# A two-layer hybrid decoder on one core: parameter columns laid out by the host, loads and lower parts in order of use, one softplus chain in layer 0

## The chip, the cores and the metric

The kernel runs on one core of a Trainium2 chip. The metric is device microseconds for one launch; the program builds in one piece and is executed several times. A core has five engines with an instruction queue each, worked off in order: TensorE (PE, matmuls and transposes, with its weight loads PEld), VectorE (DVE), ScalarE (ACT), GpSimd (POOL) and SyncE (SP, which here only issues loads and stores). The engines wait for one another on semaphores.

## The reference

Two layers, each of three sub-layers between a norm in front and a norm behind, over 256 tokens of width 1024 in f32:

```
h = rms_norm(x, pre_mix_g);   x += rms_norm(mixer(h) , post_mix_g)
h = rms_norm(x, pre_cross_g); x += rms_norm(cross(h, rms_norm(mem)), post_cross_g)
h = rms_norm(x, pre_ffn_g);   x += rms_norm((silu(h@w_gate) * (h@w_up)) @ w_down, post_ffn_g)
```

The mixer projects h with one matrix `w_in` (1024 x 3080) whose columns belong to three head groups. The RG-LRU group runs a short convolution, two gates and a linear recurrence whose decay is `exp(-8 * r * softplus(-lambda))`. The forgetting attention adds to its logits the differences of `c = cumsum(log_sigmoid(f + b_f))`, one f per token and head (8 heads). The retention group rotates q and k by position and weights the scores by a fixed decay. The three outputs are concatenated and multiplied by `w_out`. `log_sigmoid(z)` is `-softplus(-z)`, so the f of both token tiles and lambda all pass through a softplus.

## The kernel before, in words

The 256 tokens are two tiles of 128 (t = 0 and 1). All large products are made in three passes of a rounded format: an f32 operand is split into an upper part (`hi`, a cast on ACT) and a lower part (`lo = raw - hi`, a subtraction on DVE, or on POOL for two pieces of the beginning), and `mm3` (L355) issues hi·hi, hi·lo and lo·hi. The normed activations are split likewise: `flip_half` (L601) transposes four 128-column blocks of x on PE, multiplies them by a gain column on DVE (`xg`), casts on ACT (`xth`), and `rest` (L611) subtracts on DVE (`xtl`). The factor of the norm per token (`rs`) is applied after the product, so the products need only the gains.

Weights stream through five raw buffers (`RAW_BUFS`, 1056 columns each) and eight pairs of split buffers. `load` (L423) issues the next load on SP as soon as the raw buffer's lower part has been taken, and `pump` (L433) issues the next split. The plan of pieces begins, in layer 0, with `fv_hi` (264 columns, four pieces of two k-blocks), `fk` (512 columns, four pieces), `lru` (four), `fv_lo` (two), `fq`, `rqk` and `rvg` (four each).

Everything is emitted by one Python program that carries a clock per engine, `Flow` (L117): each instruction is charged a duration (`Engine.cost`, L238, and `matmul`, L308), and side tasks (generators that were spawned) are resumed between two `mm3` as soon as the model says that what they wait for is ready. So the duration table sets where transposes, softmax pieces and small products stand in the queues of all engines, for the whole program.

The beginning before the change: SP loads a first part of a packed constant array (`cst`: identity, 16 rows of pre_mix gains, the forget bias and the inverse frequencies, 304 columns), x of tile 0 in two halves, two weight pieces, x of tile 1 in one load, and the other pieces. PE warms up on zeros (`busy`, L1163), transposes the 16 gain rows into columns (`cols`), then the blocks of x. In `project` (L481) each k-block's three passes follow one another. `second_tile` (L1186) flips tile 1 and then issues on POOL five loads: a second part of `cst` (triangle, ones and 72 more parameter rows), the mask, the third part of `cst` (1024 KB) and the two memory tiles (512 KB each). `setup_rest` (L1129) transposes the 72 rows and runs the softplus of lambda, four columns wide. `use_fv_hi` (L700) runs a softplus, eight columns wide, for the f of each tile, and multiplies its result with triangle and ones on PE (`cum`), on which the keys and queries of the attention wait (`augmented`, L719). A softplus is 15 dependent instructions on DVE, fourteen of them behind one Exp on ACT.

At a layer's end `post` normalises the last product of a tile, adds it to x, and flips x for the next sub-layer; PE meanwhile works on what it has.

Of the kernel before, what the change touches and what calls it, by code (L numbers as in the profile page):

```python
# [15 lines left out]
ALU = mybir.AluOpType  # L16
# [28 lines left out]

C_ID, C_R1, C_BF, C_INV, C_FIRST = 0, 128, 256, 272, 304
C_TRI, C_ONE, C_R2, C_SOON = 304, 432, 560, 688
C_DEC, C_BD, C_END = 688, 1712, 2736


G_MIX = 0
N_FIRST = 16
G_MEM, G_CROSS, G_FFN = 16, 24, 40
L_CW, L_CB, L_BR, L_BI, L_LAM = 56, 72, 76, 80, 84
N_ROWS = 88

# [15 lines left out]
def _pack(inp):  # L72

    (eye, tri, ones, dec, inv), mask = _constants()
    pack = np.zeros((P, C_END), np.float32)
    pack[:, C_ID:C_ID + P] = eye
    pack[:, C_TRI:C_TRI + P] = tri
    pack[:, C_ONE:C_ONE + P] = ones
    pack[:, C_DEC:C_BD] = dec
    pack[:, C_INV:C_FIRST] = inv  # L80
    pack[0:N_FIRST, C_R1:C_R1 + P] = inp["pre_mix_g"].reshape(-1, P)
    for r0, name in ((G_MEM, "mem_norm_g"), (G_CROSS, "pre_cross_g"), (G_FFN, "pre_ffn_g"), (L_CW, "conv_w"),
                     (L_CB, "conv_b"), (L_BR, "b_rg"), (L_BI, "b_ig"), (L_LAM, "lru_lambda")):
        v = inp[name].reshape(-1, P)
        pack[r0 - N_FIRST:r0 - N_FIRST + v.shape[0], C_R2:C_R2 + P] = v
# [31 lines left out]
class Flow:  # L117
# [6 lines left out]
    def __init__(self):  # L124
        self.clock = {"PE": 0.0, "ACT": 0.0, "DVE": 0.0, "POOL": 0.0, "DMA": 0.0}
        self.seq, self.tasks, self.pumps, self.written, self.hold = 0, [], [], {}, 0
        self.free, self.reads, self.late = {}, {}, []
# [29 lines left out]
    def load(self, queue, out):  # L157

        if queue == "POOL":
            self.issue("POOL", 1.05, [], [])  # L160
        t = max(self.now, self.clock.get(queue, 0.0), self.free.get(out.tensor.name, 0.0)) + 1.1
        cost = out.nbytes() / 370e3
# [50 lines left out]
class Engine:  # L213
# [24 lines left out]
    def cost(self, op, outs, ins, kw):  # L238
        n = max(_size(x) for x in outs + ins[:1])
        psum = any(x.space == bass.MemoryType.PSUM for x in outs + ins)  # L240
        if self.name == "ACT":
            f = ([x for x in kw["funcs"] if x in TABLES] or [self.table])[0]
            load, self.table = 1.3 * (TABLES.get(f) != TABLES.get(self.table)), f
            return load + (0.165 if psum else 0.2) + n * 0.82e-3 + 0.19 * ("accum_out" in kw) + 0.09 * (len(ins) - 1)
        if self.name == "POOL":
# [31 lines left out]
def decoder(ctx: ExitStack, tc: tile.TileContext, a, out):  # L277
# [21 lines left out]
    def small(shape, dt=F32, n="s"):  # L299
        return sp.tile(shape, dt, tag="s", name=nm(n), bufs=64)  # L300

# [26 lines left out]
    def softplus(out_ap, x, n):  # L328

        ab, e, d, w, w2, q = (small([P, n], n=k) for k in ("ab", "e", "d", "aw", "aw2", "aq"))  # L330
        V.scalar_tensor_tensor(ab, x, -1.0, x, op0=ALU.mult, op1=ALU.max)
# [148 lines left out]

    def project(x, b):  # L481

        q = bank("acc")
        for k in range(KC):
            wh, wl = weights(b, k, NT)
# [17 lines left out]
    ident, tri, ones = (cst[:, c:c + P] for c in (C_ID, C_TRI, C_ONE))  # L503
    rows1, rows2 = cst[0:N_FIRST, C_R1:C_R1 + P], cst[0:N_ROWS - N_FIRST, C_R2:C_R2 + P]
    bf = cst[:, C_BF:C_INV].rearrange("p (l h) -> p l h", l=DEPTH)
# [4 lines left out]
    minus_half = const([P, 4], n="mh")  # L510
    cols = const([P, N_ROWS], n="cols")
    posi = const([P, NT], I32, n="posi")
    cosb, sinb = const([P, NT, 32], n="cos"), const([P, NT, 32], n="sin")
    spl, hb = const([P, 8], n="spl"), const([P, 8], n="hb")
    sp2, sp4 = spl[:, 0:4], spl[:, 4:8]

    SY.dma_start(out=cst[:, 0:C_FIRST], in_=a["pack"][:, 0:C_FIRST])
    for c in range(2):
        SY.dma_start(out=X[0][:, 512 * c:512 * c + 512], in_=a["x"][0, 0:P, 512 * c:512 * c + 512])
    load(2)  # L520
    SY.dma_start(out=X[1], in_=a["x"][0, P:2 * P, :])
    load(RAW_BUFS)
# [170 lines left out]
    def mixer(l, xt, blk, skew):  # L693
# [6 lines left out]
        def use_fv_hi(t, q):  # L700
            S.activation(v[t][:, 256:512], q[:, 0:256], AF.Copy, bias=0.0, scale=rs[t])
            z, lf[t], cum[t] = small([P, 8], n="z"), small([P, 8], n="lf"), small([P, 8], n="cum")
# [5 lines left out]
            for s in range(t + 1):  # L708
                matmul(b[:, 0:8], tri if s == t else ones, lf[s], s == 0, s == t)
            V.tensor_copy(cum[t], b[:, 0:8])  # L710
            got["cum", t] = 1

# [415 lines left out]

    def setup_rest():  # L1129
        tb = bank("tr")  # L1130
        transpose(tb[:, 0:N_ROWS - N_FIRST], rows2)
        V.tensor_copy(cols[:, N_FIRST:N_ROWS], tb[:, 0:N_ROWS - N_FIRST])
        neg = small([P, 4])
        V.tensor_scalar(neg, cols[:, L_LAM:L_LAM + 4], -1.0, None, op0=ALU.mult)
        yield from softplus(sp2, neg, 4)
        PO.tensor_scalar(sp4, sp2, -4.0, None, op0=ALU.mult)
        PO.tensor_scalar(sp2, sp2, -2.0, None, op0=ALU.mult)
        V.tensor_scalar(hb, cols[:, L_BR:L_BR + 8], 0.5, None, op0=ALU.mult)

    def memory_norm(m):  # L1140
# [113 lines left out]
```

## Time and profile before

| | |
|---|---|
| median of 3 runs | 852.02 us (851.98 to 853.30) |
| the profiled execution: its own time | 851.84 us |
| its span, from first to last instruction | 850.1 us |
| PE busy | 838.3 us, 99% of the span |
| DVE, ACT, POOL busy | 556.5, 436.4, 77.0 us |
| mean granted PE clock | 0.997 |

Rows of a timeline give start, duration, engine, line, operation, output<-inputs, and in brackets how long the engine stood idle before it and what released it. A row with xN merges N instructions of the same kind. Matmuls are pipelined: a row's duration holds its latency too, so the distance between the starts of two rows is what PE takes for one.

### The profile page before, as it was taken

The numbers are of one execution on the slowest core, as the hardware profiler recorded it, in microseconds if no ns is written. First come the engines' busy times: TensorE is split into PE (matmuls) and PEld (weight loads), VectorE is DVE, ScalarE is ACT, GpSimd is POOL, SyncE is SP. The second block draws the span as 40 slices with busy tenths as digits, with TensorE's granted clock in tenths as the row PEclk, the third lists the DMA queues.
The fourth block names the chain that finished last, engine by engine and source line by source line (L and its number), as shares of the span: only waits on it lengthen the run. The fifth ranks groups of instructions, "written<-read, shape, count | busy, mean of one in ns | idle before, by whom it ended". The sixth has DMA issues, their size and how long they took to land.

```text
span 850.1 us, 13415 instructions
## 1 busy us (share of the span) xinstructions
PE 838.3 (99%) x5328; PEld 751.0 (88%) x5329; DVE 556.5 (65%) x812; ACT 436.4 (51%) x666; POOL 77.0 (9%) x121
## 2 busy tenths in 40 slices
PE   7999999999999999999999999999999999999997
PEld 5888998999889999999888889889988899999995
DVE  5877886865577655557585775687566874656552
ACT  5479565645456434435355764465455653534431
POOL 2831211100020000000010201010001100000000
PEclk9999999999999999999999999999999999999999
DMA  8863525763457747546435523646443676657411
GB/s 270 302 221 106 174 76 174 216 205 100 149 155 258 234 140 229 188 137 227 145 99 173 173 81 119 223 148 227 146 151 101 221 243 202 198 143 232 146 51 50
DMA packets 92623, 145.25 MB, mean 171 GB/s; under 512 B 4768, under 2 KB 62240, under 8 KB 92432
## 3 DMA queue, kind: packets, MB, share of 16 engines
q1 hardware_dynamic: 91120, 138.65, 51.2%
q0 software_dynamic: 1440, 5.74, 1.9%
q8 instruction: 42, 0.69, 0.3%
q14 instruction: 21, 0.17, 0.1%
HBM read 143.32 MB, written 1.05 MB: 170 GB/s over the span
## 4 chain that ended last, share of the span: by engine, by line
PE 96%; issue 1%; DMA 1%; DVE 0%; SPq 0%; ACT 0%; DVEq 0%; POOLq 0%; POOL 0%; ACTq 0%
PE acc L309 61%; PE dn L309 24%; PE tr L321 4%; PE lg L309 2%; PE clg L309 1%; PE co L309 1%; PE fo L309 1%; DMA raw<-in_w_in 1%; PE ry L309 1%; PE rsc L309 1%; SPq L229 0%; PE gate L309 0%; DVE xg L234 0%; ACT xth L234 0%; DVE lo L234 0%
## 5 line engine op out<-in xcount | busy, mean ns | idle before, releaser
L234 DVE TENSOR_TENSOR lo<-raw,hi 128x1024 fp32r<-128x1024 f32 (+1 forms) x244 | 292.0, 1219 | 151.1 <-ACT hi L234 150.3
L234 ACT CAST hi<-raw 128x1024 fp32r<-128x1024 f32 (+2 forms) x246 | 251.5, 1043 | 137.4 <-PE acc L309 93.7
L309 PE MATMUL acc<-xth,hi 128*128 128x256 f32 x704 | 198.9, 282 | 0.0
L309 PE MATMUL acc<-xth,lo 128*128 128x256 f32 x704 | 198.6, 282 | 0.0
L309 PE MATMUL acc<-xtl,hi 128*128 128x256 f32 x704 | 197.7, 281 | 0.0
L309 PEld LDWEIGHTS acc<-xth,hi 128*128 128x128 f32 x704 | 133.1, 189 | 0.8
L309 PEld LDWEIGHTS acc<-xtl,hi 128*128 128x128 f32 x704 | 133.0, 189 | 0.8
L309 PEld LDWEIGHTS acc<-xth,lo 128*128 128x128 f32 x704 | 133.1, 189 | 0.0
L309 PE MATMUL acc<-hi,xth 128*128 128x512 f32 (+2 forms) x288 | 111.5, 387 | 2.4 <-ACT xth L234 2.3
L309 PE MATMUL acc<-lo,xth 128*128 128x512 f32 (+2 forms) x288 | 106.9, 371 | 1.2 <-DVE lo L234 0.8
L309 PE MATMUL acc<-hi,xtl 128*128 128x512 f32 (+2 forms) x288 | 107.1, 372 | 0.2 <-DVE xtl L234 0.2
L309 PEld LDWEIGHTS acc<-hi,xth 128*128 128x128 f32 x288 | 54.9, 191 | 11.6 <-ACT xth L234 3.0
L309 PEld LDWEIGHTS acc<-hi,xtl 128*128 128x128 f32 x288 | 54.6, 190 | 10.3 <-DVE xtl L234 0.7
L309 PEld LDWEIGHTS acc<-lo,xth 128*128 128x128 f32 x288 | 55.0, 191 | 9.6 <-DVE lo L234 1.0
L234 POOL TENSOR_TENSOR rp<-ssp,mh 128x1 f32<-128x1 f32 x12 | 6.7, 560 | 545.2 <-DVE ssp L234 545.2
L309 PE MATMUL dn<-hi,mth 128*128 128x512 f32 x128 | 51.1, 399 | 0.0
L309 PE MATMUL dn<-hi,mtl 128*128 128x512 f32 x128 | 50.5, 394 | 0.0
L309 PE MATMUL dn<-lo,mth 128*128 128x512 f32 x128 | 50.4, 393 | 0.0
L309 PE MATMUL dn<-hi,gh 128*128 128x512 f32 x112 | 44.2, 395 | 0.0
L309 PE MATMUL dn<-hi,gl 128*128 128x512 f32 x112 | 44.1, 394 | 0.0
L309 PE MATMUL dn<-lo,gh 128*128 128x512 f32 x112 | 44.1, 393 | 0.0
L234 DVE TENSOR_TENSOR y<-dn,gpost 128x512 f32<-128x512 f32 x24 | 16.4, 686 | 34.1 <-ACT junk L234 34.1
(228 smaller groups left out, 1369.9 us busy)
## 6 DMA issues: line engine op xcount, KB each, us to landing
raw<-in_w_in SPq DMA_DIRECT2D x44, 512.0 KB, 4.5
raw<-in_w_gate SPq DMA_DIRECT2D x44, 512.0 KB, 4.5
raw<-in_w_up SPq DMA_DIRECT2D x44, 512.0 KB, 4.7
raw<-in_w_down SPq DMA_DIRECT2D x44, 512.0 KB, 4.5
raw<-in_w_ck SPq DMA_DIRECT2D x16, 512.0 KB, 4.4
raw<-in_w_out SPq DMA_DIRECT2D x16, 512.0 KB, 4.2
raw<-in_w_cv SPq DMA_DIRECT2D x16, 512.0 KB, 5.2
raw<-in_w_cq SPq DMA_DIRECT2D x16, 512.0 KB, 5.0
```

Source lines behind the costliest of these rows:

```text
L234: fn(*args, **kw)
L309: nc.tensor.matmul(out_ap, lhsT, rhs, start=start, stop=stop)
L321: nc.tensor.transpose(out_ap, src, ident[0:k, 0:k])
```

## The change

The host now lays all 88 parameter columns into `cst` as columns (C_COLS), so both transposes of parameter rows and the copies behind them go. The first load of `cst` has 136 columns (identity and pre_mix gains); the 384 columns of the second part (the other parameters, forget bias, frequencies, triangle, ones) are loaded on SP behind the fourth weight piece, not on POOL. x of tile 1 comes in two halves. In the beginning the lower parts are all made on DVE, two of them ahead of or between the lower parts of x, and the two uppers come first on ACT. `project` for the first product works piece by piece: both k-blocks hi·hi, then hi·lo, then lo·hi. In layer 0 the softplus of lambda and of both tiles' f is one chain on 20 columns, spawned with tile 1, and the three `cum` products follow it together; layer 1 keeps a chain for each tile. The duration table of `Flow` is lowered: DVE by 0.075 us for most instructions, ACT by 0.065 us, the hand-over between engines from 0.15 to 0.12 us, and the first loads are charged 270 instead of 370 KB per us.

```
-    def issue(self, engine, cost, outs, ins, latency=0.15):
+    def issue(self, engine, cost, outs, ins, latency=0.12):
...
-            return load + (0.165 if psum else 0.2) + n * 0.82e-3 + 0.19 * ("accum_out" in kw) + 0.09 * (len(ins) - 1)
+            return load + (0.1 if psum else 0.135) + n * 0.82e-3 + 0.19 * ("accum_out" in kw) + 0.09 * (len(ins) - 1)
...
-        return 0.155 + n * (0.6e-3 if one else 1.06e-3) + 0.06 * (op == "scalar_tensor_tensor" and not psum)
+        return 0.08 + n * (0.6e-3 if one else 1.06e-3) + 0.06 * (op == "scalar_tensor_tensor" and not psum)
...
+        for k0 in range(0, KC if staged else 0, b.per):
+            ks = range(k0, k0 + b.per)
+            w = {k: weights(b, k, NT) for k in ks}
+            for i, j in ((0, 0), (0, 1), (1, 0)):
+                for k in ks:
+                    matmul(q[:, 0:b.n], x[i][:, k, :], w[k][j], k + i + j == 0, k == KC - 1 and i == 1)
+                flow.tick()
...
-    load(2)
-    SY.dma_start(out=X[1], in_=a["x"][0, P:2 * P, :])
+    for t in range(NT):
+        for c in range(2):
+            cut = slice(512 * c, 512 * c + 512)
+            SY.dma_start(out=X[t][:, cut], in_=a["x"][0, t * P:t * P + P, cut])
+        load(2 + 2 * t)
+    SY.dma_start(out=cst[:, C_FIRST:C_SOON], in_=a["pack"][:, C_FIRST:C_SOON])
...
-            yield from softplus(lf[t], z, 8)
+            if skew:
+                yield from softplus(lf[t], z, 8)
+            elif t == 0:
+                return
+            else:
+                yield [cst[:, C_FIRST:C_SOON], z]
+                V.tensor_scalar(zs[:, 0:4], cols[:, L_LAM:L_LAM + 4], -1.0, None, op0=ALU.mult)
+                yield from softplus(lfs, zs, 20)
+                PO.tensor_scalar(sp4, lfs[:, 0:4], -4.0, None, op0=ALU.mult)
...
-    def setup_rest():
...
-    pump(True, lows)
+    for _ in range(2):
+        pump(True, lows)
     second = flip_half(nrm[0], X[0], G_MIX, 1)
     busy(WARM2)
+    lows[0](V)
     rest(*first)
-    lows[0](V)
+    lows[1](V)
     rest(*second)
-    for eng in (PO, V, PO):
-        pump(True, lows)
-        lows[-1](eng)
...
-        PO.dma_start(out=cst[:, C_FIRST:C_SOON], in_=a["pack"][:, C_FIRST:C_SOON])
...
-    flow.spawn(setup_rest(), rows2)
```

Place 1 is the beginning. On ACT, before: the four uppers of `fv_hi` (raw_86 to raw_93) and the first of `fk` (raw_95) all stand ahead of the two casts of tile 1 (xg_187, xg_200).

```order
L234 CAST hi_129<-raw_86 128x528
L234 CAST xth_99<-xg_137 128x512
L234 CAST hi_149<-raw_88 128x528
L234 CAST hi_155<-raw_91 128x528
L234 CAST hi_161<-raw_93 128x528
L234 CAST hi_177<-raw_95 128x1024
L234 CAST xth_99<-xg_187 128x512
L234 CAST xth_99<-xg_200 128x512
```

On ACT now: the third piece of `fv_hi` is raw_92, the fourth raw_94; tile 1's products are xg_177 and xg_189.

```order
L230 CAST hi_128<-raw_86 128x528
L230 CAST hi_133<-raw_88 128x528
L230 CAST xth_101<-xg_141 128x512
L230 CAST hi_167<-raw_92 128x528
L230 CAST xth_101<-xg_177 128x512
L230 CAST xth_101<-xg_189 128x512
L230 CAST hi_194<-raw_94 128x528
```

The casts of tile 1 moved ahead of the fourth upper and of the first `fk` piece. On DVE at the same place, before:

```order
L234 TENSOR_TENSOR lo_156<-raw_91,hi_155 128x528
L234 TENSOR_TENSOR lo_178<-raw_95,hi_177 128x1024
L234 TENSOR_TENSOR xg_187<-tr_182,cols_77 128x512
L234 TENSOR_TENSOR xg_200<-tr_195,cols_77 128x512
L234 TENSOR_TENSOR xtl_100<-xg_187,xth_99 128x512
L234 TENSOR_TENSOR xtl_100<-xg_200,xth_99 128x512
```

On DVE now, from the third lower part on:

```order
L230 TENSOR_TENSOR lo_168<-raw_92,hi_167 128x528
L230 TENSOR_TENSOR xg_177<-tr_172,cst_74 128x512
L230 TENSOR_TENSOR xg_189<-tr_184,cst_74 128x512
L230 TENSOR_TENSOR xtl_102<-xg_177,xth_101 128x512
L230 TENSOR_TENSOR xtl_102<-xg_189,xth_101 128x512
L230 TENSOR_TENSOR lo_195<-raw_94,hi_194 128x528
L230 TENSOR_TENSOR lo_208<-raw_97,hi_207 128x1024
```

Tile 1 now stands between the third and the fourth lower part, where before it stood behind the first lower part of `fk`; the second and fourth lower parts, which POOL made before, are on DVE.

Place 2 is the softplus of layer 0 on DVE. Before, the chain of tile 0 (e_281 to lf_276) follows the last lower part of `lru` (lo_368), and the chain of tile 1 follows it:

```order
L234 TENSOR_TENSOR lo_368<-raw_225,hi_367 128x1024
L234 TENSOR_SCALAR d_282<-e_281 128x8
L234 RECIPROCAL d_282<-d_282 128x8
L234 TENSOR_TENSOR aw_283<-e_281,d_282 128x8
L234 TENSOR_TENSOR aw_284<-aw_283 128x8
L234 TENSOR_SCALAR aq_285<-aw_284 128x8
L234 SCALAR_TENSOR_TENSOR aq_285<-aq_285,aw_284 128x8 x7
L234 SCALAR_TENSOR_TENSOR aq_285<-aq_285,aw_283 128x8
L234 SCALAR_TENSOR_TENSOR lf_276<-z_275,aq_285 128x8
```

Now the one chain (all its tiles are called soft_82) begins with lambda behind the last lower part of `lru` (lo_346), and its main part stands behind the first lower part of `fv_lo` (lo_377, of raw_281, the thirteenth piece):

```order
L230 TENSOR_TENSOR lo_346<-raw_262,hi_345 128x1024
L230 TENSOR_SCALAR soft_82<-cst_74 128x4
L230 SCALAR_TENSOR_TENSOR soft_82<-soft_82 128x20
L230 TENSOR_SCALAR aug_357<-acc_305,rstd_119 128x8x64
L230 MEMSET aug_357 128x8
L230 TENSOR_TENSOR lo_377<-raw_281,hi_376 128x1024
L230 TENSOR_SCALAR soft_82<-soft_82 128x20
L230 RECIPROCAL soft_82<-soft_82 128x20
```

One wide chain moved behind one more weight piece than the narrow ones had in front of them. On PE the three `cum` products stand together behind 75 matmuls of 512 columns (`fk` and `lru`); before, the first stood behind 72 and the other two behind 90.

Place 3 is PE at the change of layers, where tile 1's x is transposed (tr) for layer 1 while PE works on tile 0's `fk`, before tile 1's first product (acc_4642 before and acc_4573 now, 264 columns). Before:

```order
L321 MATMUL tr_4597<-cst_74,x_73 128x128 x4
L321 MATMUL tr_4605<-cst_74,x_73 128x128 x4
L309 MATMUL acc_4575<-hi_4487,xth_99 128x512
L309 MATMUL acc_4575<-lo_4488,xth_99 128x512
L309 MATMUL acc_4575<-hi_4487,xtl_100 128x512
L309 MATMUL acc_4642<-hi_4282,xth_99 128x264
```

And now:

```order
L317 MATMUL tr_4522<-cst_74,x_73 128x128 x4
L317 MATMUL tr_4530<-cst_74,x_73 128x128 x4
L305 MATMUL acc_4506<-hi_4414,xth_101 128x512
L305 MATMUL acc_4506<-lo_4415,xth_101 128x512
L305 MATMUL acc_4506<-hi_4414,xtl_102 128x512
L305 MATMUL acc_4506<-hi_4423,xth_101 128x512
L305 MATMUL acc_4506<-lo_4424,xth_101 128x512
L305 MATMUL acc_4506<-hi_4423,xtl_102 128x512
```

Three more matmuls like the last three follow before tile 1's first product, so nine matmuls, not three, stand between the transposes and it: the transposes moved up by six matmuls.

More of the change, by code (lines that the diff above doesn't have):

```diff
@@ L43 @@
 HOLD_LEAD = 1
[L46 to L53, printed above, removed]
+C_ID, C_COLS, C_FIRST = 0, 128, 136
+C_BF, C_INV, C_TRI, C_ONE, C_SOON = 216, 232, 264, 392, 520
+C_DEC, C_BD, C_END = 520, 1544, 2568
+G_MIX, G_MEM, G_CROSS, G_FFN = 0, 16, 24, 40
 L_CW, L_CB, L_BR, L_BI, L_LAM = 56, 72, 76, 80, 84
-N_ROWS = 88
 def _constants():
@@ L124, in __init__ @@
     def __init__(self):
-        self.clock = {"PE": 0.0, "ACT": 0.0, "DVE": 0.0, "POOL": 0.0, "DMA": 0.0}
+        self.clock = {"PE": 0.0, "ACT": 0.0, "DVE": 0.0, "POOL": 0.0, "DMA": 1.2}
         self.seq, self.tasks, self.pumps, self.written, self.hold = 0, [], [], {}, 0
@@ L161, in load @@
         t = max(self.now, self.clock.get(queue, 0.0), self.free.get(out.tensor.name, 0.0)) + 1.1
-        cost = out.nbytes() / 370e3
+        cost = out.nbytes() / (270e3 if self.clock["DMA"] < 8.0 else 375e3)
         if queue == "POOL":
@@ L299, in small @@
     def small(shape, dt=F32, n="s"):
-        return sp.tile(shape, dt, tag="s", name=nm(n), bufs=64)
+        return sp.tile(shape, dt, tag="s", name=nm(n), bufs=60)
     def bank(n="ps"):
@@ L328, in softplus @@
     def softplus(out_ap, x, n):
-        ab, e, d, w, w2, q = (small([P, n], n=k) for k in ("ab", "e", "d", "aw", "aw2", "aq"))
+        ab, e, d, w, w2, q = (soft[:, k, 0:n] for k in range(6))
         V.scalar_tensor_tensor(ab, x, -1.0, x, op0=ALU.mult, op1=ALU.max)
@@ L479, in weights, with project @@
         return tuple(x[:, o + lo_:o + hi_] for x in b.parts[i])
-    def project(x, b):
+    def project(x, b, staged=False):
         q = bank("acc")
-        for k in range(KC):
+        for k0 in range(0, KC if staged else 0, b.per):
[5 more added lines that the diff above has]
+                flow.tick()
+        for k in range(0 if staged else KC):
             wh, wl = weights(b, k, NT)
@@ L503, in decoder @@
     ident, tri, ones = (cst[:, c:c + P] for c in (C_ID, C_TRI, C_ONE))
-    rows1, rows2 = cst[0:N_FIRST, C_R1:C_R1 + P], cst[0:N_ROWS - N_FIRST, C_R2:C_R2 + P]
+    cols = cst[:, C_COLS:C_BF]
     bf = cst[:, C_BF:C_INV].rearrange("p (l h) -> p l h", l=DEPTH)
@@ L514, in decoder @@
     spl, hb = const([P, 8], n="spl"), const([P, 8], n="hb")
+    soft = const([P, 8, 20], n="soft")
+    zs, lfs = soft[:, 6], soft[:, 7]
     sp2, sp4 = spl[:, 0:4], spl[:, 4:8]
     SY.dma_start(out=cst[:, 0:C_FIRST], in_=a["pack"][:, 0:C_FIRST])
-    for c in range(2):
-        SY.dma_start(out=X[0][:, 512 * c:512 * c + 512], in_=a["x"][0, 0:P, 512 * c:512 * c + 512])
-    load(2)
-    SY.dma_start(out=X[1], in_=a["x"][0, P:2 * P, :])
+    for t in range(NT):
[4 more added lines that the diff above has]
+    SY.dma_start(out=cst[:, C_FIRST:C_SOON], in_=a["pack"][:, C_FIRST:C_SOON])
     load(RAW_BUFS)
@@ L539, in rotary_tables @@
         ang, n1, n2, s, s2, m = (work([P, NT, 32], n="ang") for _ in range(6))
-        inv = cst[:, C_INV:C_FIRST]
+        inv = cst[:, C_INV:C_TRI]
         for t in range(NT):
@@ L701, in use_fv_hi @@
             S.activation(v[t][:, 256:512], q[:, 0:256], AF.Copy, bias=0.0, scale=rs[t])
-            z, lf[t], cum[t] = small([P, 8], n="z"), small([P, 8], n="lf"), small([P, 8], n="cum")
+            o = 4 + 8 * t
+            z, lf[t], cum[t] = zs[:, o:o + 8], lfs[:, o:o + 8], small([P, 8], n="cum")
             V.scalar_tensor_tensor(z, q[:, 256:264], rs[t], bf[:, l, :], op0=ALU.mult, op1=ALU.add)
             V.tensor_scalar(z, z, -1.0, None, op0=ALU.mult)
-            yield from softplus(lf[t], z, 8)
+            if skew:
[7 more added lines that the diff above has]
+                PO.tensor_scalar(sp4, lfs[:, 0:4], -4.0, None, op0=ALU.mult)
+                PO.tensor_scalar(sp2, lfs[:, 0:4], -2.0, None, op0=ALU.mult)
+                V.tensor_scalar(hb, cols[:, L_BR:L_BR + 8], 0.5, None, op0=ALU.mult)
             yield lf[t]
             b = bank("cum")
[L708 to L711, printed above, removed]
+            for u in [t] if skew else range(NT):
+                at = 8 * u
+                for s in range(u + 1):
+                    matmul(b[:, at:at + 8], tri if s == u else ones, lf[s], s == 0, s == u)
+                V.tensor_copy(cum[u], b[:, at:at + 8])
+                got["cum", u] = 1
         def use_fv_lo(t, q):
@@ L974, in mixer @@
                 for name, use in group:
-                    q = project(xt[t].x, blk[name])
+                    q = project(xt[t].x, blk[name], not skew and t == 0 and name == "fv_hi")
                     flow.spawn(scaled(xt[t], use(t, q)))
@@ L1127, in decoder @@
     mem = [Norm() for _ in range(NT)]
-    def setup_rest():
[L1130 to L1138, printed above, removed]
     def memory_norm(m):
@@ L1167, in decoder @@
     busy(WARM)
-    tb = bank("tr")
-    transpose(tb[:, 0:N_FIRST], rows1)
-    V.tensor_copy(cols[:, 0:N_FIRST], tb[:, 0:N_FIRST])
     flow.pumps.append(pump)
@@ L1191, in second_tile @@
             todo.append(flip_half(nrm[1], X[1], G_MIX, c))
-            yield 0.3
+            yield X[1]
         for r in todo:
@@ L1199, in second_tile @@
             scale_norm(nrm[t], X[t], (0.5,))
-        PO.dma_start(out=cst[:, C_FIRST:C_SOON], in_=a["pack"][:, C_FIRST:C_SOON])
         PO.dma_start(out=maskb, in_=a["mask"])
         flow.spawn(late_loads())
-        flow.spawn(rotary_tables(), posi)
-        flow.spawn(setup_rest(), rows2)
+        flow.spawn(rotary_tables(), [posi, cst[:, C_FIRST:C_SOON]])
         for m in range(NT):
             flow.spawn(memory_norm(m), 1.0)
-    flow.spawn(second_tile(), X[1])
+    flow.spawn(second_tile(), X[1][:, 0:512])
     for l in range(DEPTH):
```

12 lines of the change are left out of this document (5 added, 7 removed).

## The prediction

> **What bounds the kernel now.** First the page: PE is busy nearly all the time, so a change can only pay where PE waits or runs at a lower clock.
>
> ```profile
> PE 838.3 (99%) x5328; PEld 751.0 (88%) x5329; DVE 556.5 (65%) x812; ACT 436.4 (51%) x666; POOL 77.0 (9%) x121
> ```
>
> The waits of PE from 0 to 60 us (total, times, longest) show where. These are the largest behind the warm-up; both lie before 16 us, and the larger is for tile 1's cast.
>
> ```profile
> PE acc L309 <- ACT xth L234: 2.0, 1, 2.0
> PE acc L309 <- DVE lo L234: 0.8, 1, 0.8
> ```
>
> The windows (stretch, length, busy time of PE, PEld, DVE, ACT, POOL, granted clock, DMA share, GB/s) show what followed: after a stretch in which PE was busy for 1.02 of 3.41 us, the clock was half for the next 3.4 us.
>
> ```profile
> 5.70:9.12 3.42, 2.37 (x11) 1.27 (x11) 3.39 (x6) 1.88 (x3) 0.26 (x1) 1.00 0.93 316
> 12.53:15.94 3.41, 1.02 (x7) 0.68 (x6) 2.46 (x4) 1.52 (x3) 0.46 (x1) 1.00 0.99 358
> 15.94:19.36 3.42, 3.42 (x14) 3.19 (x15) 2.48 (x3) 3.42 (x6) 0.72 (x2) 0.50 0.70 246
> ```
>
> The timeline of PE gives the cost: tile 1's first product begins at 15.92, the next block (`fk`) at 20.62, so 24 matmuls took 4.7 us; nine of them at the full clock, from 19.42 to 20.50, took 0.12 us each, and 24 would take 2.9.
>
> ```profile
> 15.92 0.59 PE L309 MATMUL acc<-hi,xth 128*128 128x264 f32 x1 [2.00 <-ACT xth L234]
> 19.42 0.28 PE L309 MATMUL acc<-hi,xtl 128*128 128x264 f32 x1
> 20.50 0.28 PE L309 MATMUL acc<-hi,xtl 128*128 128x264 f32 x1
> 20.62 0.39 PE L309 MATMUL acc<-hi,xth 128*128 128x512 f32 x1
> 29.62 0.23 PE L321 MATMUL tr<-cst 72*128 72x72 f32 x1
> ```
>
> **The start of tile 1.** The third weight piece lands when ACT's wait ends, at 10.22.
>
> ```profile
> 8.14 0.63 ACT L234 CAST hi<-raw 128x528 fp32r<-128x528 f32 x1
> 10.22 1.37 ACT L234 CAST hi<-raw 128x528 fp32r<-128x528 f32 x2 [1.45 <-DMA raw<-in_w_in]
> 15.25 1.22 ACT L234 CAST xth<-xg 128x512 fp32r<-128x512 f32 x2 [1.89 <-DVE xg L234]
> 10.89 0.71 DVE L234 TENSOR_TENSOR lo<-raw,hi 128x528 fp32r<-128x528 f32 x1 [1.67 <-ACT hi L234]
> 14.53 1.28 DVE L234 TENSOR_TENSOR xg<-tr,cols 128x512 f32<-128x512 f32 x2
> ```
>
> Ahead of it there are now 168 columns less of `cst`, 84 KB, which at the 316 GB/s above is 0.27 us: 9.95. From there the new order is one chain: upper 0.63, lower 0.71, the two xg 1.28, the second xth 0.62, the fourth upper 0.63, its lower 0.70, and some 0.3 us of hand-overs, together 4.8 us: 14.8. Four matmuls of the first product follow (0.5), and tile 1 begins at 15.2 (14.7 to 15.7, as the landing moves), 0.7 earlier. PE still waits about 2 us, now ahead of the fourth piece. Whether the clock falls is the next question: in the stretch 12.53 to 15.94 PE would be busy for about 1.6 us, between the 1.02 after which it fell and the 2.37 after which it did not. With the clock kept `fk` begins at 18.1, with the clock halved as before at 19.7, instead of 20.62. [...]
>
> **The softplus chain.** This takes part of it back. PE reaches the `cum` products after 75 matmuls of 512 columns; 39 of them took from 20.62 to 29.62, 0.231 each, so at 18.1 + 17.3 = 35.4, or 37.0 with the low clock. The chain stands on DVE behind the lower part of the thirteenth piece, so its load decides, and that one meets POOL's five (now four) loads.
>
> ```profile
> 20.26 1.06 ACT L234 ACTIVATE junk<-x 128x1024 bf16<-128x1024 f32 x1
> 17.32 1.05 ACT L234 ACTIVATE junk<-x 128x1024 bf16<-128x1024 f32 x1
> 22.81 0.77 POOL L229 DMA_DIRECT2D cst<-in_pack  x1
> ```
>
> The two squares with two uppers between are 2.94 us apart, and POOL's first load is issued 2.55 after the second. ACT is now free for the first square at 13.9, so POOL's loads begin at 19.4, 3.4 earlier. The thirteenth piece is loaded when the eighth's lower part is done, by the same durations at about 21.8, that is 2.4 us behind POOL's first load. How long such a load takes is shown by three loads of SP issued from 18 to 22 us and four from 26 to 30, the latter 3.4 us and more behind POOL's first:
>
> ```profile
> raw<-in_w_in SPq DMA_DIRECT2D x3, 512.0 KB, 4.5
> raw<-in_w_in SPq DMA_DIRECT2D x4, 512.0 KB, 9.9
> ```
>
> Between 26.3 and 31.7 I take 31.4, near the second row, as POOL's third part of `cst` and the two memory tiles, 2 MB, stand ahead. When both queues had work, from 29 to 33 us, the shares were:
>
> ```profile
> q0 software_dynamic: 305, 1.20, 76.1%
> q1 hardware_dynamic: 340, 0.35, 24.9%
> ```
>
> Then an upper of 1.05 and a lower of 1.16 (4.64 for four), 33.7, and the chain:
>
> ```profile
> 24.97 4.64 DVE L234 TENSOR_TENSOR lo<-raw,hi 128x1024 fp32r<-128x1024 f32 x4 [1.21 <-ACT hi L234]
> 29.54 0.17 DVE L234 TENSOR_SCALAR d<-e 128x8 f32<-128x8 f32 x1
> 32.40 0.17 DVE L234 SCALAR_TENSOR_TENSOR lf<-z,aq 128x8 f32<-128x8 f32 x1
> 46.56 0.16 DVE L234 TENSOR_SCALAR d<-e 128x4 f32<-128x4 f32 x1
> 49.14 0.16 DVE L234 SCALAR_TENSOR_TENSOR spl<-s,aq 128x4 f32<-128x4 f32 x1
> ```
>
> Eight columns took 3.0 us, four took 2.7; twenty are between 3.0 and, drawn on in a line, 3.9; I take 3.7. It ends at 37.4, so PE waits there for 2.0 us with the full clock and 0.4 with the low one: what the clock does no longer matters. With three products (0.6) PE is at 38.0. To compare, the same work was done before at 38.27 plus the two products that came later, 0.45 in these rows:
>
> ```profile
> 38.27 0.40 PE L309 MATMUL acc<-hi,xth 128*128 128x512 f32 x1
> 41.48 0.40 PE L309 MATMUL acc<-hi,xtl 128*128 128x512 f32 x1
> 42.08 0.48 PE L309 MATMUL acc<-hi,xth 128*128 128x512 f32 x1
> 42.39 0.39 PE L309 MATMUL acc<-lo,xth 128*128 128x512 f32 x1
> ```
>
> So 38.7 becomes 38.0: 0.7 gained. Without the wait it would be 2.7 (full clock) or 1.1 (low). The transpose of the 72 rows, 0.1 us in PE's spacing, is in the 38.7. The two narrow chains and lambda's free some 5 us of DVE, which nothing in PE waited for: no gain. Behind the chain DVE has the scaling of tile 1's keys (512 columns like an xg, 0.7), three lower parts (3.5) and small instructions (0.7) before the keys can be transposed, 4.9 us; PE has 4.5 with the three products. That is 0.4 us of wait.
>
> **The lowered durations.** They pull every side task forward. At the change of layers this gains:
>
> ```profile
> 434.66 1.42 DVE L234 SCALAR_TENSOR_TENSOR x<-y,rp,x 128x512 f32<-128x512 f32 x2
> 437.47 1.04 PE L321 MATMUL tr<-cst,x 128*128 128x128 f32 x8
> 438.81 0.40 PE L309 MATMUL acc<-hi,xtl 128*128 128x512 f32 x1
> 439.50 0.39 PE L309 MATMUL acc<-hi,xth 128*128 128x264 f32 x1 [0.30 <-ACT xth L234]
> 439.73 0.28 PE L309 MATMUL acc<-lo,xth 128*128 128x264 f32 x1
> 440.23 0.39 PE L309 MATMUL acc<-hi,xtl 128*128 128x264 f32 x1 [0.22 <-DVE xtl L234]
> ```
>
> From 438.81 to 439.50 and from 439.73 to 440.23 PE lost 0.46 and 0.38 us beyond 0.23 and 0.12. x was ready at 436.08, the transposes began at 437.47; six matmuls, 1.4 us, earlier is just when x is ready. I take 0.75 of the 0.84, with 0 and 0.84 as bounds. Elsewhere tasks may now stand too early and PE wait. The gate products of layer 0 are the likeliest:
>
> ```profile
> 50.87 1.52 DVE L234 SCALAR_TENSOR_TENSOR xc<-lxp,cols,xc 128x256 f32<-128x256 f32 x3
> 52.76 2.81 DVE L234 SCALAR_TENSOR_TENSOR xc<-lxp,cols,xc 128x256 f32<-128x256 f32 x3
> ```
>
> The same three instructions took 1.3 us longer when POOL worked beside them, and no duration table holds that. Bounds 0 and 1.3 per place; I take 0.1 in all.
>
> **The sum**, against the profiled execution's own 851.84 (span 850.1, 1.7 around it; 0.18 below the median, nothing at this scale): −0.7 up to `cum`, +0.4, −0.75, +0.1: 850.9 us.
>
> **The rivals.** *The chain is in time.* If the thirteenth load takes 4.5 us, the chain ends at 33.7 or so, before PE comes. For it speaks that the load lies between the two rows, 2.4 us behind POOL's first where the slow ones were 3.4 and more; against it that the fast ones were all issued ahead of POOL's first, at 22.81. The start is then kept: −2.7 − 0.75 + 0.1 gives 848.5 with the full clock, −1.1 gives 850.1 with the low one. [...] The row above gives SP a quarter.
>
> *Slower: waits along DVE.* If the twelfth piece is held up by POOL's loads as well, the chain begins later still, and with it spl on POOL, the keys and xc. It decides once the chain ends after about 39.5: PE is then at 40.1 after `cum` (+1.4), waits 0.4 for the keys and 1.3 at the gates, against 0.75 gained: 854.2. The rows for the xc group speak for it; that PE had no wait after 20 us in this layer speaks against.
>
> [...]
>
> **How the numbers follow.** About 0.2%, 1.7 us, is what a measurement can tell from no change: below 850.3 counts as faster, above 853.7 as slower. The forecast, chain late by one to two us, 0.52 (its own range 849.8 to 852.2); in time, 0.21; slower, 0.14; nothing, 0.13. Faster: 0.19 of the second, 0.18 of the first, 0.03 of the last, 0.40. Slower: 0.13 and 0.01. Same: 0.46. The range reaches from the case in time to short of the slower one: 848.4 to 853.6.
>
> **What would show it.** In the new profile: tile 1's first product of 264 columns near 15.2; the windows from 15 to 19 us at clock 1.00 or 0.50; POOL's first load near 19.4; the thirteenth piece's cast on ACT at 31 to 32; a wait of PE at `cum` behind DVE's soft tile of 0.4 to 2 us; no wait at 439. No wait at `cum` and a cast near 27 would make the forecast wrong in its main term; waits of over 1 us in 40 to 140 us would show the slower rival.

## The result and the profile after

The changed kernel took 860.62 us, median of 5 runs (859.98 to 861.57), against 852.99 us of the kernel before (851.98 to 853.30): a ratio of 1.0093, interval 1.0081 to 1.0105. It is slower by 7.6 us. The forecast was 850.9, range 848.4 to 853.6. The profiled execution took 859.98 us, with a span of 858.0.

The page of the changed kernel first. PE has the same work (838.3 us before); the span grew by 7.9 us.

```profile
PE 839.8 (98%) x5327; PEld 750.9 (88%) x5327; DVE 553.9 (65%) x782; ACT 436.1 (51%) x664; POOL 74.4 (9%) x118
```

The waits of PE over the whole program (total, times, longest). The first row is the new one: PE waits for a `cum` tile that DVE produces, 4.0 us at one place. Third stands the wait for the softplus chain ("issue": the page shows no releaser for it), fourth two waits at the gate products.

```profile
PE cum L305 <- DVE cum L230: 4.0, 1, 4.0
PE acc L305 <- ACT hi L230: 2.3, 2, 1.6
PE cum L305 <- issue: 1.7, 1, 1.7
PE gate L305 <- DVE xc L230: 1.6, 2, 1.0
```

PE's timeline, from the fourth weight piece to behind `cum`:

```profile
13.34 0.51 PE L305 MATMUL acc<-hi,xth 128*128 128x264 f32 x2 [1.63 <-ACT hi L230]
14.75 0.28 PE L305 MATMUL acc<-hi,xth 128*128 128x264 f32 x1
17.66 0.39 PE L305 MATMUL acc<-hi,xth 128*128 128x512 f32 x1
...
34.72 0.40 PE L305 MATMUL acc<-hi,xtl 128*128 128x512 f32 x1
36.83 0.36 PE L305 MATMUL cum<-soft,cst 128*128 128x8 f32 x2 [1.71 <-issue]
41.18 1.02 PE L305 MATMUL cum<-soft,cst 128*128 128x8 f32 x4 [3.99 <-DVE cum L230]
42.06 0.77 PE L305 MATMUL acc<-hi,xth 128*128 128x512 f32 x1
42.63 0.63 PE L305 MATMUL acc<-lo,xth 128*128 128x512 f32 x1
```

Tile 1's first product, the 24 matmuls ahead of `fk`, begins at 14.75 (15.92 before), `fk` at 17.66 (20.62 before). Up to the first `cum` product the change is ahead. Each `cum` product is two instructions, so the row with x2 is the first product and the one with x4 the other two. These two, which need nothing else from the softplus chain, begin 4.35 us behind the first. DVE's timeline shows why: the copy of the first result stands behind three lower parts.

```profile
36.33 0.39 DVE L230 SCALAR_TENSOR_TENSOR soft<-soft 128x20 f32<-128x20 f32 x2
...
36.72 0.75 DVE L230 TENSOR_SCALAR aug<-acc,rstd 128x512 f32<-128x512 f32 x1
37.39 1.21 DVE L230 TENSOR_TENSOR lo<-raw,hi 128x1024 fp32r<-128x1024 f32 x1
...
38.52 2.51 DVE L230 TENSOR_TENSOR lo<-raw,hi 128x1024 fp32r<-128x1024 f32 x2
40.98 0.15 DVE L230 COPY cum<-cum 128x8 f32<-128x8 f32 x1
```

The windows around it (length, busy time of PE, PEld, DVE, ACT, POOL, granted clock, DMA share, GB/s) show the price on top: the clock is half for two stretches of 3.4 us.

```profile
36.20:39.62 3.42, 0.36 (x2) 0.30 (x2) 3.35 (x8) 1.10 (x2) 2.58 (x4) 1.00 0.29 105
39.62:43.03 3.41, 1.85 (x6) 1.69 (x7) 1.88 (x7) 0.00 (x0) 2.90 (x7) 0.50 0.88 301
43.03:46.45 3.42, 3.42 (x10) 2.61 (x9) 1.28 (x1) 1.17 (x2) 2.91 (x7) 0.50 0.42 160
46.45:49.86 3.41, 3.41 (x27) 3.07 (x26) 1.77 (x2) 3.02 (x6) 1.00 (x3) 1.00 0.58 158
```

The account, after against before. The work that before stood at 38.7 (as the prediction worked it out) stands at 42.06: +3.3. From 42.06 to 46.45 PE did at half clock, with 0.43 us from one product of 512 columns to the next (0.23 from 46.91 on, at the full clock), what takes about half of these 4.4 us at the full clock: +2.2. The gate products cost 0.59 and 0.99 us of waiting, one pair in each layer:

```profile
60.35 0.70 PE L305 MATMUL gate<-xc,cst 128*128 128x256 f32 x2 [0.59 <-DVE xc L230]
...
476.32 0.70 PE L305 MATMUL gate<-xc,cst 128*128 128x256 f32 x2 [0.99 <-DVE xc L230]
```

The change of layers gave back what was forecast: no wait ahead of tile 1's first product, 264 columns wide, and 0.23, 0.13 and 0.12 us from row to row.

```profile
445.22 0.40 PE L305 MATMUL acc<-hi,xtl 128*128 128x512 f32 x1
445.45 0.28 PE L305 MATMUL acc<-hi,xth 128*128 128x264 f32 x1
445.58 0.28 PE L305 MATMUL acc<-lo,xth 128*128 128x264 f32 x1
445.70 0.28 PE L305 MATMUL acc<-hi,xtl 128*128 128x264 f32 x1
```

That is 0.46 and 0.38 back. 3.3 + 2.2 + 1.6 - 0.8 is 6.3 of the 7.9 us; the rest lies in pieces of a few tenths that were not followed up.

### The profile page after: what moved, and what is told of

It is laid out like the page before. It is cut to its first block, busy times and chain, and to the rows that moved or that the text cites. A ratio compares the mean times of both kernels' runs of the same rounds, so it can differ in the third digit from the quotient of the medians.

```text
span 858.0 us, 13403 instructions
## 1 busy us (share of the span) xinstructions
PE 839.8 (98%) x5327; PEld 750.9 (88%) x5327; DVE 553.9 (65%) x782; ACT 436.1 (51%) x664; POOL 74.4 (9%) x118
## 3 DMA queue, kind: packets, MB, share of 16 engines
HBM read 143.23 MB, written 1.05 MB: 168 GB/s over the span
## 4 chain that ended last, share of the span: by engine, by line
PE 91%; DMA 3%; DVE 3%; issue 2%; ACT 1%; SPq 0%; DVEq 0%; POOLq 0%; POOL 0%; ACTq 0%
PE acc L305 56%; PE dn L305 24%; PE tr L317 4%; DMA raw<-in_w_in 2%; PE lg L305 2%; PE co L305 1%; PE clg L305 1%; PE fo L305 1%; DVE xc L230 1%; DVE lo L230 1%; ACT hi L230 1%; PE ry L305 1%; DMA raw<-in_w_down 1%; PE rsc L305 1%; PE gate L305 0%
## 5 line engine op out<-in xcount | busy, mean ns | idle before, releaser
L230 DVE TENSOR_TENSOR lo<-raw,hi 128x1024 fp32r<-128x1024 f32 (+2 forms) x246 | 297.2, 1225 | 169.3 <-ACT hi L230 168.3
```

The costliest lines, as they stand in the source:

```text
L230: fn(*args, **kw)
```

## The experiments

The theory after this reading: the second `cum` product waits for the copy of the first because both tiles' results lie in one bank (the buffer that `bank("cum")` gives, into which PE writes them), and that copy is queued behind the lower parts of pieces that POOL's loads made late. The rivals: the late pieces bind anyhow; or the lowered durations carry the loss.

**e1: the three products together.**

```
-            for u in [t] if skew else range(NT):
-                at = 8 * u
+            us = [t] if skew else range(NT)
+            for u in us:
                 for s in range(u + 1):
-                    matmul(b[:, at:at + 8], tri if s == u else ones, lf[s], s == 0, s == u)
-                V.tensor_copy(cum[u], b[:, at:at + 8])
+                    matmul(b[:, 8 * u:8 * u + 8], tri if s == u else ones, lf[s], s == 0, s == u)
+            for u in us:
+                V.tensor_copy(cum[u], b[:, 8 * u:8 * u + 8])
```

> The changed kernel with one edit: the three cum products are issued one after the other, and the two copies behind them; nothing else moves. Theory (the second product waits for the copy of the first, because both tiles' results lie in one bank, and that copy is queued on DVE behind three lower parts): the wait of 4.0 us goes. The scaled keys stay where they were on DVE, ready near 41.7, and PE reaches their transposes near 40.8, so some 0.9 us of wait comes back there. The half clock from 39.6 to 46.4 (2.1 us) goes too. 860.6 - 4.1 + 0.9 - 2.1 = 855.3 us (854.0 to 856.5). Rival (DVE and the weight pieces are simply late at that place, and PE waits as long for the next thing it needs): 859.5 to 860.6.

Measured: 854.68 us (853.86 to 856.04), 1.0036 of before [1.0023, 1.0049], about 6 us less than the changed kernel. That lies in the theory's range, and the rival falls. The 0.9 us of wait at the keys that the theory added did not come, so a part of the agreement is luck. PE's timeline in e1: the six rows of `cum` are one group and the next product follows 0.66 us behind; the wait for the chain (1.7) is still there.

```profile
38.60 0.81 PE L305 MATMUL cum<-soft,cst 128*128 128x8 f32 x6 [1.66 <-issue]
39.26 0.47 PE L305 MATMUL acc<-hi,xth 128*128 128x512 f32 x1
```

The half clock from 39.6 to 46.4 is gone too; the window of e1 over the later part of it has the clock at 1.00:

```profile
42.00:46.40 4.40, 4.40 (x29) 3.70 (x28) 4.40 (x9) 3.40 (x7) 4.06 (x5) 1.00 1.01 339
```

**e13: a bank for each tile, products and copies in the changed kernel's order.**

```
             b = bank("cum")
+            bs = {u: bank("cum") for u in ([t] if skew else range(NT))}
             for u in [t] if skew else range(NT):
-                at = 8 * u
+                b, at = bs[u], 0
```

> The changed kernel with a bank of its own for each token tile's cum, products and copies in the changed kernel's order. Theory (the second product waited for the copy only because it shares the bank with it): the wait of 4.0 us goes as in e1, 854.7 us (853.5 to 856.0). Rival (it is the order, product then copy then product, that makes PE wait, whatever the bank): 860 to 861.

Measured: 854.5 us (853.69 to 857.24), 1.0033 [1.0019, 1.0046]. The same as e1, with the order left alone:

```profile
37.52 0.81 PE L305 MATMUL cum<-soft,cst 128*128 128x8 f32 x6 [2.18 <-issue]
```

So it is the shared bank: with one bank the product that writes columns 8 to 16 waited 3.99 us for the reader of columns 0 to 8, with a bank for each the six rows are one group without that wait. Whether the chip itself would need that order within one bank, no run tells.

**e8: POOL's loads later, DVE's order unchanged.**

```
-        PO.dma_start(out=cst[:, C_DEC:C_END], in_=a["pack"][:, C_DEC:C_END])
-        for t in range(NT):
-            PO.dma_start(out=msrc[t], in_=a["mem"][0, t * P:(t + 1) * P, :])
+        todo = [(cst[:, C_DEC:C_END], a["pack"][:, C_DEC:C_END])]
+        todo += [(msrc[t], a["mem"][0, t * P:(t + 1) * P, :]) for t in range(NT)]
+        for out, _ in todo:
+            flow.load("POOL", out)
+        yield 9.0
+        for out, src in todo:
+            PO.eng.dma_start(out=out, in_=src)
```

> The changed kernel with POOL's three large loads (part of the constants and the two memory tiles, 2 MB) issued some 6 us later, behind the first steps of the angles on POOL; DVE's order is unchanged. Theory (the thirteenth weight load took 10.3 us because POOL's loads stood before it, and everything on DVE hangs on it): it lands near 26, the chain ends near 32, no wait at the first cum product, lower parts and copies end near 36 instead of 41, so 1 us is left of the 4.0, and the clock stays: 860.6 - 1.9 - 3.1 - 2.1 = 853.5 us (852.5 to 855). Rival (the load is slow for SP's own queue, which has five loads in flight): landing stays past 30, 859.5 to 861.

Measured: 856.14 us (854.16 to 859.05), 1.0051 [1.0031, 1.0071]: 4.5 us less than the changed kernel, with 7.1 expected. The profiled execution took 854.76 us, inside the theory's range, and the median lies 1.1 us above it. The fall of the clock near 15 us doesn't explain that, since this execution had it too (half clock from 14.5 to 17.9 us). The two longer of the four executions, 857.52 and 859.05, show a mean granted clock of 0.995 and 0.993, against 0.997 here; what lowered it there stays open. The mechanism is in the rows. The thirteenth weight load, issued at 21, as the DMA view of the changed kernel gives it (KB, us from issue to landing):

```profile
raw<-in_w_in SPq DMA_DIRECT2D x1, 512.0 KB, 10.3
```

and as that of e8 gives it:

```profile
raw<-in_w_in SPq DMA_DIRECT2D x1, 512.0 KB, 5.5
```

In e8's timeline PE no longer waits ahead of the first `cum` product (the row has no bracket), and 0.37 of the 3.99 us is left ahead of the second:

```profile
36.78 0.28 PE L305 MATMUL cum<-soft,cst 128*128 128x8 f32 x2
37.43 0.61 PE L305 MATMUL cum<-soft,cst 128*128 128x8 f32 x4 [0.37 <-DVE cum L230]
```

**e2: e1, and the chain at once behind its Exp.** `yield e` in `softplus` is passed over for the 20 columns.

> As e1, and the softplus chain goes on at once behind its exponential, ahead of the lower part of the thirteenth piece instead of behind it. Theory (the 1.9 us ahead of the first cum product are the thirteenth load, which arrives at 31.4 and holds the chain): the chain begins near 26.9 and ends near 30, PE reaches cum without a wait, and 1.9 us more go than in e1; the keys are then scaled near 35 and their wait goes as well: 855.3 - 1.9 - 0.9 = 852.5 us (851.0 to 853.5). Rival (the late loads bind anyway: PE takes the wait at the first product that needs the thirteenth or a later piece): 854.5 to 856.

Measured: 853.25 us (852.2 to 855.6), 1.0017 [1.0006, 1.0028]. Inside the theory's range, 1.4 us less than e1; the wait of 1.7 at `cum` is gone (the row has no bracket). The other 0.9 us that the theory took off stood for the wait at the keys, which e1 doesn't have either. PE's timeline:

```profile
32.71 0.73 PE L305 MATMUL cum<-soft,cst 128*128 128x8 f32 x6
```

**e3: idle products in the wait.** Between the first and the second `cum` product:

```
+                if u and not skew:
+                    fb = bank("fill")
+                    for _ in range(16):
+                        nc.tensor.matmul(fb[:, 0:P], tri, ones, start=True, stop=True)
```

> The changed kernel with 16 idle products of 128 columns, into a bank of their own, between the first and the second cum product, where PE waits for 4.0 us; no result of them is used. They take the place of waiting, not of work. Theory (the clock fell from 39.6 to 46.4 because PE stood, and that cost 2.1 us on top of the wait): the wait stays, the clock stays at 1.00, and the time is 860.6 - 2.1 = 858.5 us (858.0 to 859.2). Rival (the slow matmuls from 42 to 46 cost nothing, since PE would have waited for DVE's keys at their end): 860.2 to 861.0.

Measured: 859.37 us (857.5 to 860.37), 1.0087 [1.0071, 1.0102]: 1.2 us less than the changed kernel, just above the theory's range, and the intervals overlap. The medians alone settle nothing. The two profiled executions, both with the full clock at 16 us, took 857.5 and 859.98 us, 2.5 apart with 2.1 expected, but that is one execution of each. The windows of e3 do show the clock kept at the same wait:

```profile
36.70:40.80 4.10, 3.94 (x34) 3.87 (x34) 4.10 (x7) 0.63 (x2) 3.64 (x5) 1.00 0.27 57
40.80:43.00 2.20, 1.88 (x11) 1.58 (x11) 0.73 (x6) 0.31 (x1) 1.82 (x5) 1.00 1.05 398
```

**e9: the gate products later.** One line in `lru`, behind `yield xc`:

```
+            yield 1.2
```

> The changed kernel with one pause of 1.2 us in the plan ahead of the gate products of each layer, so that they stand some six matmuls later on PE. Theory (these products stand too early behind xc because of the lowered durations, 0.75 and 1.16 us): both waits go, nothing else changes: 860.6 - 1.9 = 858.7 us (858.0 to 859.5). Rival (the order behind is tight, and the wait moves on to the next side task): 860 to 863.

Measured: 859.84 us (859.18 to 861.75), 1.0098 [1.0083, 1.0113]; no gain that can be told from none. The waits at the gates are gone from e9's waits, as the theory said, but this profile lost its clock at 16 us, which the changed kernel's kept (below). Inconclusive by itself; e10 uses it.

**The durations: e4, e5, e6, e7.** Four kernels that swap the table. e4 is the kernel before with the new table, e5 the changed kernel with the old one (the edit is the lines of the table in the diff), e6 is e2 with the old one, and e7 has the old one and the narrow chains, so of the change only the beginning.

> The kernel before with the lowered durations alone: no new loads, no staged start, narrow softplus chains. Theory (the table gives 0.84 us at the change of layers and takes 0.75 and 1.16 us at the gate products of the two layers, which stand too early behind xc): 853.0 - 0.84 + 1.9 = 854.1 us (853.5 to 854.6). Rival (layer 0's gate wait in the changed kernel was only a consequence of its late beginning, and layer 1's of nothing in the table): 852.2 us.

> The changed kernel with the durations of before. Theory (the loss is in the wide chain and the shared bank of cum, and the durations only place the gate products too early): the waits at cum stay, the copies stand behind four lower parts; the waits of 0.75 and 1.16 us at the gate products go, and the 0.84 us of the change of layers come back: 860.6 - 1.9 + 0.8 = 859.5 us (858.5 to 861). Rival (e4 was 12.8 us slower with the durations alone, so they carry the changed kernel's loss too): 852 us or less.

> e2 (chain ahead of the thirteenth piece's lower part, three cum products together) with the durations of before. Theory: against e2 the gate waits of 1.03 and 1.15 us and those of 0.5 and 0.4 us in the two feed-forward blocks go, 0.84 us at the change of layers come back: 853.25 - 3.1 + 0.8 = 851.0 us (849.8 to 852.0), the first version not slower than before. Rival (these waits have nothing to do with the durations): 853.5 to 854.1.

> The new beginning alone: columns from the host, loads in order of use, staged first product, with the separate narrow softplus chains (8, 8 and 4 columns) and the durations of before. Theory (the start gains what the forecast gave it, 2.7 us with the clock kept at 16 us or 1.1 without, and the wide chain took it back): 851.9 - 1.1 to - 2.7 = 849.2 to 850.8. Rival (the beginning gives nothing that lasts, the next loads bind): 851.9.

Measured: e4 864.63 us (863.01 to 866.25), 1.0151 [1.0136, 1.0166]; e5 864.47 (861.5 to 868.65), 1.0159 [1.0130, 1.0188]; e6 858.87 (857.92 to 864.2), 1.0095 [1.0073, 1.0117]; e7 860.24 (857.66 to 863.47), 1.0102 [1.0084, 1.0121]. All four are outside of what the theory and the rival expected. Each has a long wait of its own that neither kernel has; the first row of e5 is the changed kernel's wait again. From the waits of PE behind 20 us, of e4:

```profile
PE rsc L309 <- DVE rw L234: 3.1, 1, 3.1
```

of e5:

```profile
PE cum L305 <- DVE cum L230: 4.6, 1, 4.6
PE rsc L305 <- DVE rw L230: 3.0, 1, 3.0
```

of e6:

```profile
PE acc L305 <- DVE meml L230: 6.0, 1, 6.0
```

and of e7:

```profile
PE acc L305 <- DVE lo L230: 2.8, 1, 2.8
PE dn L305 <- ACT mth L230: 2.7, 1, 2.7
```

What follows: table and beginning can't be priced one without the other, since a table puts every side task of the program in another place. The gain at the change of layers does belong to the table (e5 and e6 have the two waits of 0.3 and 0.2 us there again), and so do the gate waits (e5 and e6 have none). What the beginning is worth by itself, these four don't tell.

**e10 to e12, e14: repairs.** e10 puts together e1, e8 and e9.

> The changed kernel with three repairs: cum products together (e1), POOL's three large loads later (e8), gate products later (e9). Theory (these are the places where the changed kernel loses, and they add): e8's profile was 2.2 us behind the kernel before at its end; 0.5 us at cum and 1.9 at the gates go: 852.1 - 0.2 = 851.9 us (850.8 to 853.0), with 1.6 us more or less as the clock at 15 us falls or not. Rival (the waits aren't independent, a repaired place shows the next): 854 to 856.

Measured: 852.11 us (850.29 to 853.27), 1.0002 [0.9993, 1.0011]: as the theory had it. The named places carry the loss. In e10 PE's waits from 20 to 500 us are two of 0.2 us.

e11 adds idle products ahead of the fourth piece, in `project`:

```
+            if k0 == 6:
+                fb = bank("fill")
+                for _ in range(7):
+                    nc.tensor.matmul(fb[:, 0:P], ident, ident, start=True, stop=True)
```

> e10 with seven idle products of 128 columns, into a bank of their own, where PE waits 1.8 us for the fourth weight piece near 12 us; no result of them is used. Theory (the clock at 15 us falls in some executions and not in others after that wait; filled, it never falls): no half clock from 14 to 19 us, 1.0 to 1.6 us less than e10 and less spread: 850.6 us (849.6 to 851.6). Rival (what is gained there is lost again at the next late piece, as the forecast had it at cum): the same as e10.

Measured: 850.6 us (849.94 to 851.39), 0.9986 [0.9978, 0.9995], the first version faster than the kernel before, and the spread is half of e10's. The windows behind the wait, of e10 and of e11:

```profile
16.20:19.70 3.50, 3.50 (x19) 3.50 (x18) 2.92 (x3) 3.50 (x6) 2.59 (x4) 0.54 0.73 230
```

```profile
15.90:19.40 3.50, 3.50 (x26) 3.24 (x25) 2.92 (x3) 3.50 (x6) 2.59 (x4) 1.00 0.74 221
```

e12 is e10 with e2's early chain.

> e10 with the softplus chain at once behind its exponential, as in e2. Theory (with POOL's loads late the chain is in time, so its place no longer matters): within 0.5 us of e10. Rival (the chain still holds PE): 1 to 2 us less than e10.

Measured: 855.02 us (854.68 to 855.52), 1.0040 [1.0024, 1.0055]. A miss on both sides, 3 us more than e10: the early chain moved the plan, and PE now waits 1.5 us for a softmax piece of the attention (`pexp`, on ACT) ahead of 99 us, and the clock is half for the 3.4 us behind it:

```profile
99.06 0.50 PE L305 MATMUL acc<-hi,xth 128*128 128x512 f32 x1 [1.48 <-ACT pexp L230]
```

```profile
96.81:100.22 3.41, 1.93 (x12) 1.56 (x12) 1.81 (x4) 2.23 (x7) 0.00 (x0) 1.00 0.90 269
100.22:103.63 3.41, 3.41 (x14) 2.82 (x13) 1.83 (x2) 1.51 (x4) 0.00 (x0) 0.50 0.31 61
```

e14 asks whom e11's gain belongs to: the kernel before, with eight such products ahead of tile 1's first one.

> The kernel before with eight idle products of 128 columns, into a bank of their own, where PE waits 2.0 us for tile 1's cast near 14 us; no result of them is used. It tells how much of what e11 gained over the kernel before belongs to the filled wait and not to the change. Theory (the half clock after that wait costs the kernel before 1.8 us): 851.95 - 1.8 = 850.2 us (849.5 to 850.9), so that the repaired change is worth nothing of its own. Rival (PE waits for the next late piece instead, since before's loads aren't in order of use): 851.5 to 852.

Measured: 850.49 us (849.7 to 851.19), 0.9984 [0.9975, 0.9993]. The same as e11: filling one wait of 2 us gives the kernel before what the repaired and filled change has. The kernel before also runs that fast without any edit at times: of its 62 executions beside these experiments, the six with a mean granted clock of 0.999 took 850.19 to 851.48 us, the others 851.03 to 853.84. The first matmul of `fk`, in PE's timeline of e10, of e11 and of e14:

```profile
19.74 0.40 PE L305 MATMUL acc<-hi,xth 128*128 128x512 f32 x1
```

```profile
17.94 0.39 PE L305 MATMUL acc<-hi,xth 128*128 128x512 f32 x1
```

```profile
18.72 0.39 PE L309 MATMUL acc<-hi,xth 128*128 128x512 f32 x1
```

The profiles' spans (847.9 for e11, 848.7 for e14) differ by the 0.8 us of the last two; the medians don't show it. So the change, with its faults mended, is worth less than the measurement can tell.

## Why the prediction was wrong

**The start of tile 1: right.** Forecast 15.2 for tile 1 and 18.1 for `fk` with the clock kept, measured 14.75 and 17.66. The wait moved ahead of the fourth piece as written, 1.63 instead of about 2 us. Whether the clock falls behind it differs from execution to execution: kept in the changed kernel's profile, fallen in e10's.

**The softplus chain: right up to its end.** POOL's first load was issued at 19.50 (19.4). The thirteenth load took 10.3 us; its cast began at 31.46 (31.4 forecast for the landing), as ACT's timeline has it:

```profile
31.46 1.05 ACT L230 CAST hi<-raw 128x1024 fp32r<-128x1024 f32 x1 [4.39 <-DMA raw<-in_w_in]
```

The chain ended at 36.7 (37.4), and PE waited 1.7 us for it (2.0). e8 shows the reason given, POOL's loads ahead of it.

**Where it failed: "With three products (0.6) PE is at 38.0."** The sum took the three `cum` products as standing together, as the order listed them, and charged them 0.6. They took from 36.83 to 42.06, 5.2 us. The copy between the first and the second was in the diff, in one loop over one bank, but the step left out that it ties PE to DVE's queue, behind three lower parts that run one after the other, 3.6 us in all, and only once the late chain has ended. e1 and e13 remove the tie in two ways and gain 6 us each.

**The clock behind it: left out.** "What the clock does no longer matters" was about the fall at 16 us, and held only roughly: the first `cum` product began at 37.81 in e9 and at 38.60 in e1, whose clock fell there, against 36.83, with 0.6 and 0.3 of that from a beginning that ran later as a whole. Behind the new wait it was half from 39.6 to 46.4, and 1.00 in e3, where that wait was filled: 2.2 us that stand in no term.

**The keys: no wait came.** Forecast +0.4, for keys that stand behind lower parts on DVE. In the changed kernel PE itself was late, and in e1, where it wasn't, there is no such wait either. The queue of lower parts had been seen; what it would hold up was the copy, 4 us earlier.

**The change of layers: right**, 0.84 against 0.75. **Elsewhere: too small**, 0.1 taken, 1.6 measured at the two gate places, each within the bound of 1.3 that the text gave; the likeliest place was named, and then not charged. The bound came from xc beside POOL's work. In the kernel before POOL was busy beside both groups of layer 0, for 1.29 of the 1.52 us and 2.36 of the 2.81, and in layer 1 for 1.78 of 2.66 us beside the slower one and not at all beside the one of 1.53.

**The rivals.** "Slower: waits along DVE" had the sign and the engine, but another mechanism: it decides once the chain ends after 39.5, and the chain ended at 36.7. Its gate waits came; its main wait came from a copy, not from the chain. In the first rival, 33.7 for the end of the chain is 1.5 us more than the forecast's own terms give (26.3 + 1.05 + 1.16 + 3.7 = 32.2); both lie before PE comes, so nothing hangs on it. SP's quarter (24.9% from 29 to 33 us) had spoken against that rival, and the load took 10.3 us. The case "nothing", to which the forecast gave 0.13, is near what e10 and e14 say in the end. Of the 3 us that `fk` begins earlier, most is the clock, which an execution keeps or not: with the clock fallen `fk` began at 20.62 before and at 19.74 in e10, with the wait filled at 18.72 in e14 and at 17.94 in e11. By these two pairs the rebuilt beginning itself is worth 0.8 to 0.9 us, a rough figure: each pair is one execution of either kernel, and the same beginning with the clock fallen had `fk` anywhere from 19.18 (e12) to 19.82 (e9). e10 has given it back by the end, in pieces that were not followed.

## What to carry to other kernels

Read a loop of small products and copies on one bank as a round trip through the copying engine's queue, and price it by what stands in that queue ahead of the copy (3.6 us here), not by the products. Add to a wait of PE the half clock that may follow: 3.4 us of it stood behind waits of 2.00 us in the kernel before, 1.63 in e10 and 1.48 in e12, and none behind the first wait of 1.63 in the changed kernel. Try idle products there: in the kernel before that alone was worth 1.4 us. In a program whose order comes from a table of durations, a part of a change can't be priced by swapping the table, since four such swaps each brought a new wait of about 3 to 6 us.

## What the runs showed of the hardware

The stretches of half clock lasted 3.4 us in the kernel before (15.94 to 19.36) and in e10 (16.0 to 19.4), 6.8 in the changed kernel (39.62 to 46.45), and 17.1 in e4 (104.2 to 121.3), behind a single wait of 3.1 us. In e7 the clock averaged 0.87 from 100 to 140 us, which makes about 10 us at half. In e4 PE was busy for 15.80 of the 17.10 us, and for all of the 12.0 us from 108 to 120, at half clock:

```profile
104.20:121.30 17.10, 15.80 (x77) 15.04 (x78) 10.71 (x21) 5.61 (x15) 1.21 (x1) 0.50 0.37 113
121.30:125.00 3.70, 3.70 (x34) 3.70 (x34) 0.40 (x1) 0.00 (x0) 0.00 (x0) 1.00 0.00 0
```

The same wait of 1.63 us had half clock behind it in e10, and not in the changed kernel. In e10, ahead of the fall at 16.0, PE was busy for 1.81 of 3.40 us:

```profile
12.60:16.00 3.40, 1.81 (x12) 1.60 (x13) 2.11 (x5) 3.40 (x7) 0.86 (x3) 1.00 1.03 366
```

In the changed kernel PE was busy for 1.48 of 3.41 us in a stretch around the wait and for 2.08 in one that begins 0.91 us later, and the clock stayed at 1.00 up to 39.62:

```profile
11.40:14.81 3.41, 1.48 (x10) 1.05 (x9) 2.61 (x5) 3.27 (x6) 0.29 (x2) 1.00 1.06 377
12.31:15.72 3.41, 2.08 (x15) 1.87 (x15) 2.20 (x4) 3.41 (x6) 1.12 (x3) 1.00 0.99 361
```

So PE's busy time alone does not say where the point lies. Nor do e12 and e3 give it: e12's window of 96.81 to 100.22, busy for 1.93 us, lost the clock, and e3's of 11.82 to 15.23, busy for 1.90, kept it:

```profile
11.82:15.23 3.41, 1.90 (x13) 1.69 (x14) 2.14 (x4) 3.41 (x7) 0.94 (x3) 1.00 1.05 369
```

What decides in each case, and what kept e4's clock down so long, stays open.
